# The causal mask as a third matmul, and a LayerNorm that reads PSUM, in a hybrid decoder layer

## The chip, the cores and the metric

The kernel runs on one core of one Trainium2 chip. The metric is the device time of one execution in microseconds; the time before is the median of three runs. The engines are called PE (matrix products and transposes; PEld is its loading of weights), DVE (the vector engine), ACT (activations), POOL (GpSimd) and SP (the queue that issues most of the transfers).

## The reference

One decoder layer over 2048 tokens of width 1024, in float32. Half of the mixer is a convolution branch, the other half is an attention without softmax; a SwiGLU follows.

```python
glu = val * jax.nn.sigmoid(gate)                    # 512 channels
y = causal depthwise convolution of glu, width 31, + conv_b
y = _layernorm(y, ln_g, ln_b)                       # over the 512 channels
conv_out = jax.nn.silu(y)

z = einsum("bhqd,bhkd->bhqk", q, k) / 8             # 8 heads of 64
mask = key_pos < q_pos                              # a token does not read itself
log_beta, log_1m_beta = log_sigmoid(z), where(mask, log_sigmoid(-z), 0)
between = reverse_cumsum(log_1m_beta) - log_1m_beta
attn = where(mask, exp(log_beta + between), 0)      # = sigmoid(z) * prod of (1 - sigmoid)
attn_out = headwise_rmsnorm(attn @ v)

h = x + rmsnorm(concat(conv_out, attn_out) @ w_out)
h = h + rmsnorm(swiglu(rmsnorm(h)) @ w_down)        # hidden width 2816
```

## The kernel before

Tokens are worked on in four groups `g` of 512. Products keep float32 accuracy by splitting each operand into a high and a low part (`H` on ACT, `L` as the difference on DVE or POOL) and adding three matmuls into one PSUM bank.

**The first 1510 us or so** hold three streams that are recorded side by side. The dense stream is the list `PLAN`: `qkv` and `gv` (input projection, `dense`, L253, L255, L257), `out` (output projection, L684 to L686), and the first products of the feed-forward part (`c11` and `p4`, L755). Beside it run `attn` and `taps` (the convolution: 31 multiply-adds on DVE for each block of channels, L468 and L473, in a PSUM bank of the tag `cv`), each to the share of its work that `ATTN` and `TAPS` name for a place in the plan. After about 1510 us only feed-forward products are left, all on L755.

**The attention** sweeps each head's keys in chunks of 512 from the diagonal back. One score step (`scores`) handles 128 queries against one chunk: two matmuls (L558, L559) fill a bank `z`, of which there are two; ACT takes two sigmoids of it (`om` on L564, `A` on L566); DVE turns `om` into a running product (the scan on L568); POOL multiplies the two (L569). One chunk later (`values`) PE transposes `A` (L585), ACT and DVE split it (`TH` on L245, `TL` on L246) and two matmuls add to `o` (L590, L591). The scan reads one element of `z` as an operand, so the bank is held from its first matmul to the end of the scan. In a chunk on the diagonal the step is only as wide as the keys that can be seen, 128 to 512, and DVE adds -1e30 to the upper triangle of its last 128 columns (L561) before ACT reads it. There are 320 steps: 32 for group 0 (all on the diagonal), 64, 96 and 128 for the others, 32 on the diagonal in each; so 128 masks in all. Below, steps are counted from 0 in the order in which they stand on PE.

**The convolution's end** (`convnorm`) takes 128 tokens at a time, 16 times in all: PE turns the block into the `cv` bank (L486, name `lps`), ACT copies the bank to the tile `cy` (L488), DVE takes mean and variance from the copy (L490, L492), POOL makes the inverse root (L188, L189), DVE subtracts the mean and multiplies by the gain (L494), then multiplies by the inverse root and adds the offset (L495). Four score steps later PE turns the result back through the same bank (L503, `cps`); there is one `cv` bank.

What is recorded is then sorted for each engine by the framework's scheduler, which plays the program through on estimated durations; only the taps and the late feed-forward part are held in the recorded order. So each engine runs a fixed list, and an edit in one place can move rows in the lists of all of them.

Of the kernel before, what the change touches and what calls it, by code (L numbers as in the profile page):

```python
# [9 lines left out]
F32 = mybir.dt.float32  # L10
F32R = mybir.dt.float32r
BF16 = mybir.dt.bfloat16
AF = mybir.ActivationFunctionType
ALU = mybir.AluOpType
# [4 lines left out]
P = 128  # L19
# [116 lines left out]
def layer_kernel(ctx: ExitStack, tc: tile.TileContext, x, xT, g_pre_mix, w_in, conv_w, conv_b, ln_g, ln_b,  # L136
                 attn_g, w_out, g_post_mix, g_pre_ffn, w_gate, w_up, w_down, g_post_ffn, out):
    nc = tc.nc
# [7 lines left out]
    idr = cp.tile([P, P], F32R, name="idr")  # L146
# [9 lines left out]
    def const(pool, name, src, shape):  # L156
        t = pool.tile(shape, F32, name=name)
        waiting.append((t, src))
        return t
# [12 lines left out]
    def ev(name, dt=F32, n=G):  # L172
        return rp.tile([P, n], dt, tag="ev", name=name, bufs=4)
# [10 lines left out]
    def rstd_of(dst, ss, n, tag="ms"):  # L184

        w = dst.shape[-1]
        m = sp.tile([P, 8], F32, tag=tag, name=tag, bufs=4)
        nc.gpsimd.tensor_scalar(m[:, 0:w], ss, 1.0 / n, EPS, ALU.mult, ALU.add)  # L188
        nc.gpsimd.tensor_tensor(dst, m[:, 0:w], nhalf[:, 0:w], ALU.pow)  # L189
# [69 lines left out]
    def to_col(rows, k, Hs, Ls, g, banks=bank):  # L259

        ps = banks("tps")
        for t in range(TT):
# [10 lines left out]
    cc = ctx.enter_context(tc.tile_pool(name="mixconsts", bufs=1))  # L273
# [9 lines left out]
    lng = const(cc, "lng", ln_g.partition_broadcast(P), [P, CH])  # L283
# [3 lines left out]
    ident = ev("ident")[:, 0:P]  # L287
    make_identity(nc, ident)
    nc.vector.tensor_copy(idr, ident)
    msk = cc.tile([P, P], F32, name="msk")  # L290
    nc.gpsimd.memset(msk, NEG)
    nc.gpsimd.affine_select(msk, msk, pattern=[[1, P]], compare_op=ALU.is_ge, fill=0.0, base=0,
                            channel_multiplier=-1)
    one = cc.tile([P, 1], F32, name="one")
    nc.gpsimd.memset(one, 1.0)

# [163 lines left out]
    def taps(g):  # L460

        acc = vp.tile([P, CB, G], F32, tag="acc", name="acc", bufs=1)
        conv[g] = dp.tile([P, CB, G], F32, name=f"conv{g}")
        for c in range(CB):
            yield need(("val", g, c))
            a = pp.tile([P, G], F32, tag="cv", name="cv", bufs=1)
            tc.keep_in_program_order(
                nc.vector.tensor_scalar(a, gl[c][:, 0:G], cw[:, c, 0:1], cb_[:, c:c + 1], ALU.mult, ALU.add))  # L468
            yield 1
            for k in range(1, CW):  # L470
                to = acc[:, c, :] if k == CW - 1 else a
                tc.keep_in_program_order(
                    nc.vector.scalar_tensor_tensor(to, gl[c][:, k:k + G], cw[:, c, k:k + 1], a, ALU.mult, ALU.add))  # L473
                yield 1
            done.add(("taps", g, c))
        for _ in range(TAPLAG):
            yield 3
        yield from convnorm(g, acc)

    def convnorm(g, acc):  # L480

        for t in range(TT):
            ts_ = slice(t * P, (t + 1) * P)
            ps = pp.tile([P, G], F32, tag="cv", name="lps", bufs=1)
            for c in range(CB):
                nc.tensor.transpose(ps[:, c * P:(c + 1) * P], acc[:, c, ts_], id32)  # L486
            y = vp.tile([P, CH], F32, tag="cy", name="cy", bufs=1)
            nc.scalar.activation(y, ps, AF.Copy)  # L488
            st = sp.tile([P, 6], F32, tag="st", name="st")
            nc.vector.bn_stats(st, y)  # L490
            mv = sp.tile([P, 3], F32, tag="mv", name="mv")
            nc.vector.bn_aggr(mv[:, 0:2], st)  # L492
            rstd_of(mv[:, 2:3], mv[:, 1:2], 1, "msc")
            nc.vector.scalar_tensor_tensor(y, y, mv[:, 0:1], lng, ALU.subtract, ALU.mult)  # L494
            nc.vector.scalar_tensor_tensor(y, y, mv[:, 2:3], lnb, ALU.mult, ALU.add)  # L495
            s = vp.tile([P, CH], F32, tag="cs", name="cs", bufs=1)
            nc.scalar.activation(s, y, AF.Sigmoid)
            nc.gpsimd.tensor_tensor(s, y, s, ALU.mult)
            for _ in range(LAG):
                yield 3  # L500
            pt = pp.tile([P, G], F32, tag="cv", name="cps", bufs=1).rearrange("p (c t) -> p c t", c=CB)
            for c in range(CB):
                nc.tensor.transpose(pt[:, c, :], s[:, c * P:(c + 1) * P], id32)  # L503
            r = s.rearrange("p (c t) -> p c t", c=CB)
            nc.scalar.activation(r, pt, AF.Copy)
            nc.scalar.dma_start(conv[g][:, :, ts_], r)
        done.add(("conv", g))
# [22 lines left out]
    def attn(g):  # L530
# [20 lines left out]
        def scores(u, j):  # L551
            hd_ = heads[u["h"]]
            diag = u["c"] == g
            w = (j + 1) * P if diag else G
            K = u["K"]
            z = pp.tile([P, G], F32, tag="z", name="z")
            js = slice(j * P, (j + 1) * P)
            nc.tensor.matmul(z[:, 0:w], hd_["QL"][:, js], K[:, 0:w], start=True, stop=False)  # L558
            nc.tensor.matmul(z[:, 0:w], hd_["QH"][:, js], K[:, 0:w], start=False, stop=True)  # L559
            if diag:  # L560
                nc.vector.tensor_tensor(z[:, w - P:w], z[:, w - P:w], msk, ALU.add)  # L561
            om = ap.tile([P, G + 1], F32, tag="om", name="om", bufs=NOM)
            nc.gpsimd.tensor_copy(om[:, G:G + 1], hd_["prev"][j])
            nc.scalar.activation(om[:, G - w:G], z[:, 0:w], AF.Sigmoid, scale=-0.125)  # L564
            a = ap.tile([P, G], F32, tag="A", name="A", bufs=NA)
            nc.scalar.activation(a[:, 0:w], z[:, 0:w], AF.Sigmoid, scale=0.125)  # L566
            r = om[:, G - w:G + 1][:, ::-1]
            nc.vector.tensor_tensor_scan(r, r, z[:, 0:1].to_broadcast([P, w + 1]), one, ALU.mult, ALU.bypass)  # L568
            nc.gpsimd.tensor_tensor(a[:, 0:w], a[:, 0:w], om[:, G - w + 1:G + 1], ALU.mult)  # L569
            pv = sp.tile([P, 1], F32, tag="pv", name="pv", bufs=8)  # L570
            nc.gpsimd.tensor_copy(pv, om[:, G - w:G - w + 1])
            hd_["prev"][j] = pv
            u["A"].append(a)
            return w
# [56 lines left out]
        for n in range(len(units) + 1):  # L631
            u = None
            if n < len(units):
                h, c = units[n]
                if c == g:
                    yield need(("q", g, h // 2), ("k", g, h // 2), ("v", g, h // 2))
                    heads[h] = begin(h)
                u = fetch(h, c)
            for i in range(TT):
                w = 0  # L640
                if u is not None:
                    w += scores(u, i)
                if last is not None:
                    w += values(last, i)
                later = [(k - 1, fn, a) for k, fn, a in later]
                while later and later[0][0] <= 0:
                    _, fn, a = later.pop(0)
                    if fn is back and g > 1:
                        yield need(("mix", g - 2))
                    fn(a)  # L650
                yield w
            if last is not None and last["c"] == 0:
                h = last["h"]
                oT = ap.tile([P, G], F32, tag="oT", name="oT", bufs=1)
                nc.scalar.activation(oT, heads[h]["o"], AF.Copy)
                heads[h]["oT"] = oT
                later.append((FOLD, fold_halves, h))
                if h % 2:
                    later.append((BACK, back, h))
            last = u  # L660
# [721 lines left out]
```

## Time and profile before

| | before |
|---|---|
| median of 3 runs | 2632.16 us (2631.33 to 2634.64) |
| the profiled execution, and its span | 2632.4 us, 2630.6 us |
| mean granted PE clock | 0.97 |
| PE, DVE, ACT, POOL busy (share of the span) | 94%, 71%, 49%, 56% |
| first and last score step | 88.0 us, 1503.2 us |
| data moved | 657.32 MB, 250 GB/s |

A busy PE is the time in which at least one matmul is under way; matmuls overlap, so a record is longer than the distance to the next one. The granted clock is 1 when PE runs at its full rate and 0.5 when the throttle halves it. In a table of stretches each engine's number is its busy time within the stretch, and in brackets the instructions.

### The profile page before, as it was taken

To read this page: it belongs to the slowest core of one execution; us is meant where nothing else is said; L and a number is where in the kernel's file an instruction comes from. 1 tells how busy PE (TensorE), PEld (TensorE's weight loads), DVE (VectorE), ACT (ScalarE), POOL (GpSimd) and SP (SyncE) were. 2 spreads that over 40 slices of the span, in tenths; PEclk is the share of its full clock that TensorE was granted. 3 is DMA by queue.
4 is the path that set the end of the run, shared out by engine and by line. 5 is a ranking of instruction groups with operands and counts; after the bars stand their busy time and mean duration, and the time that the engine had idled before them with its cause. 6 is when DMAs were issued, how large, how long until landed. Compare 5 with 4: busy or idle time off the path is not lost.

```text
span 2630.6 us, 35776 instructions
## 1 busy us (share of the span) xinstructions
PE 2460.1 (94%) x11156; PEld 1970.1 (75%) x11156; DVE 1859.7 (71%) x2409; ACT 1290.7 (49%) x2395; POOL 1482.0 (56%) x1844
## 2 busy tenths in 40 slices
PE   8889989997999999999999989889999999999998
PEld 6777867785777778777788767667777777887886
DVE  5787569977999676687765538877776665557556
ACT  4455546656564565557666643333322224444543
POOL 6654587557765656548534406675534434557556
PEclk9999989998999999989999989999999999999999
DMA  9999869986798788856777646887665557668654
GB/s 343 330 305 308 286 221 314 358 285 219 255 350 262 251 306 277 293 168 224 264 255 231 203 152 216 315 270 242 206 210 184 193 199 271 194 196 271 210 190 170
DMA packets 289182, 657.32 MB, mean 250 GB/s; under 512 B 33888, under 2 KB 42080, under 8 KB 288992
## 3 DMA queue, kind: packets, MB, share of 16 engines
q1 hardware_dynamic: 264704, 622.01, 70.8%
q10 hardware_dynamic: 24288, 33.04, 3.5%
q8 instruction: 88, 1.44, 0.2%
q14 instruction: 102, 0.84, 0.1%
HBM read 460.92 MB, written 193.99 MB: 249 GB/s over the span
## 4 chain that ended last, share of the span: by engine, by line
PE 61%; DVE 15%; DMA 10%; POOL 6%; issue 5%; ACT 2%; SPq 1%; POOLq 0%; DVEq 0%; ACTq 0%
PE b L755 16%; PE dps L755 13%; PE c L755 9%; DVE om L568 3%; PE at L585 3%; DVE cv L473 2%; PE inps L253 2%; PE inps L255 2%; PE inps L257 2%; PE p L755 2%; PE o L591 2%; PE z L558 2%; PE ops L686 1%; PE ops L684 1%; PE ops L685 1%
## 5 line engine op out<-in xcount | busy, mean ns | idle before, releaser
L569 POOL TENSOR_TENSOR A<-A,om 128x512 f32<-128x512 f32 (+2 forms) x320 | 314.4, 983 | 356.5 <-DVE om L568 314.8
L568 DVE TENSOR_TENSOR_SCAN om<-om,one,z 128x513 f32<-128x513 f32 (+2 forms) x320 | 351.5, 1112 | 115.1 <-ACT A L566 103.1
L1061 POOL TENSOR_TENSOR wL<-raw,wH 128x512 fp32r<-128x512 f32 x176 | 257.2, 1489 | 283.7 <-ACT wH L1060 283.7
L473 DVE SCALAR_TENSOR_TENSOR cv<-glu,cw,cv 128x512 f32<-128x512 f32 x464 | 346.4, 746 | 5.8
L1241 DVE TENSOR_TENSOR xL__22087<-t__22089,xH__22086 128x512 fp32r<-128x512 f32 x154 | 197.8, 1293 | 159.2 <-ACT xH__22086 L1240 159.2
L1239 POOL TENSOR_TENSOR xL__22085<-t__22088,xH__22084 128x512 fp32r<-128x512 f32 x154 | 207.6, 1353 | 176.1 <-ACT xH__22084 L1238 175.5
L253 PE MATMUL inps<-xH,wL 128*128 128x512 f32 x640 | 262.2, 410 | 4.3 <-DVE qkL L246 4.0
L255 PE MATMUL inps<-xH,wH 128*128 128x512 f32 x640 | 259.0, 405 | 0.0
L257 PE MATMUL inps<-xL,wH 128*128 128x512 f32 x640 | 258.6, 405 | 0.0
L564 ACT ACTIVATE om<-z 128x512 f32<-128x512 f32 (+2 forms) x320 | 171.0, 536 | 164.9 <-DVE z L561 67.3
L246 DVE TENSOR_TENSOR TL<-at,TH 128x512 fp32r<-128x512 f32 (+1 forms) x320 | 189.2, 598 | 85.4 <-ACT TH L245 84.7
L755 PE MATMUL dps<-xH__22084,xL__22087 128*128 128x512 f32 x616 | 241.6, 392 | 6.8 <-DVE xL__22087 L1241 5.6
L755 PE MATMUL dps<-xL__22085,xH__22086 128*128 128x512 f32 x616 | 241.3, 392 | 3.9 <-POOL xL__22085 L1239 3.9
L755 PE MATMUL dps<-xH__22084,xH__22086 128*128 128x512 f32 x616 | 241.0, 391 | 0.0
L839 POOL TENSOR_TENSOR sum<-sum 128x512 f32<-128x512 f32 x132 | 172.2, 1305 | 104.3 <-DMA sum<-in_w_down_dram 37.5
L207 ACT ACTIVATE wH<-raw 128x1024 fp32r<-128x1024 f32 x156 | 165.6, 1062 | 104.1 <-DMA raw<-in_w_in_dram 42.7
L245 ACT ACTIVATE TH<-at 128x512 fp32r<-128x512 f32 (+1 forms) x320 | 167.7, 543 | 90.8 <-PE at L585 82.5
L1238 ACT ACTIVATE xH__22084<-t__22088 128x512 fp32r<-128x512 f32 x154 | 97.1, 631 | 232.8 <-POOL xL__22085 L1239 145.0
L585 PE MATMUL at<-idr,A 128*128 128x128 f32 x1088 | 194.2, 283 | 10.9 <-ACT ma L625 3.6
L585 PEld LDWEIGHTS at<-idr,A 128*128 128x128 f32 x1088 | 143.7, 146 | 48.8 <-POOL A L569 5.9
L566 ACT ACTIVATE A<-z 128x512 f32<-128x512 f32 (+2 forms) x320 | 167.5, 537 | 21.3 <-PE at L585 19.6
L558 PE MATMUL z<-K,QL 128*128 128x512 f32 (+2 forms) x320 | 132.4, 415 | 29.4 <-DVE om L568 24.0
(303 smaller groups left out, 6283.3 us busy)
## 6 DMA issues: line engine op xcount, KB each, us to landing
wL<-wL SPq DMA_DIRECT2D x156, 512.0 KB, 4.7
raw<-in_w_in_dram SPq DMA_DIRECT2D x80, 512.0 KB, 5.9
t__22089<-u SPq DMA_DIRECT2D x154, 256.0 KB, 2.8
c<-c ACTq DMA_DIRECT2D x88, 256.0 KB, 3.9
t__22088<-wd SPq DMA_DIRECT2D x88, 256.0 KB, 2.9
K<-kd SPq DMA_DIRECT2D x80, 256.0 KB, 4.5
V<-vd SPq DMA_DIRECT2D x80, 256.0 KB, 4.1
u<-accf SPq DMA_DIRECT2D x22, 768.0 KB, 4.1
```

The costliest lines, as they stand in the source:

```text
L246: nc.vector.tensor_tensor(L, ps, H.bitcast(F32), ALU.subtract)
L253: nc.tensor.matmul(ps, WL[:, kc], aH[t](k), start=k == 0, stop=False)
L255: nc.tensor.matmul(ps, WH[:, kc], aH[t](k), start=False, stop=False)
L257: nc.tensor.matmul(ps, WH[:, kc], aL[t](k), start=False, stop=k == KT - 1)
L473: nc.vector.scalar_tensor_tensor(to, gl[c][:, k:k + G], cw[:, c, k:k + 1], a, ALU.mult, ALU.add))
L568: nc.vector.tensor_tensor_scan(r, r, z[:, 0:1].to_broadcast([P, w + 1]), one, ALU.mult, ALU.bypass)
L569: nc.gpsimd.tensor_tensor(a[:, 0:w], a[:, 0:w], om[:, G - w + 1:G + 1], ALU.mult)
L585: nc.tensor.transpose(pt[:, j * P:(j + 1) * P], u["A"][j][:, b * P:(b + 1) * P], id32)
L755: return nc.tensor.matmul(ps, a, b, skip_group_check=True, **flags)
L1061: nc.gpsimd.tensor_tensor(l, t, f32(h), sub)
L1239: nc.gpsimd.tensor_tensor(WL, w, f32(WH), sub)
L1241: nc.vector.tensor_tensor(UL, t, f32(UH), sub)
```

## The change

The mask becomes an operand of PE. It is built in a short-lived tile, rounded once to PE's format (`mskr`), and a third matmul with the identity `idr` as the other operand adds it into the last 128 columns of the bank; the addition on DVE goes. In `convnorm` the copy to `cy` goes, and the statistics and the first of the two DVE operations read the PSUM bank `lps`.

```diff
-    msk = cc.tile([P, P], F32, name="msk")
+    mskr = cc.tile([P, P], F32R, name="mskr")
+    msk = ev("msk")[:, 0:P]
     nc.gpsimd.memset(msk, NEG)
     nc.gpsimd.affine_select(msk, msk, pattern=[[1, P]], compare_op=ALU.is_ge, fill=0.0, base=0,
                             channel_multiplier=-1)
+    nc.vector.tensor_copy(mskr, msk)
...
             y = vp.tile([P, CH], F32, tag="cy", name="cy", bufs=1)
-            nc.scalar.activation(y, ps, AF.Copy)
             st = sp.tile([P, 6], F32, tag="st", name="st")
-            nc.vector.bn_stats(st, y)
+            nc.vector.bn_stats(st, ps)
             mv = sp.tile([P, 3], F32, tag="mv", name="mv")
             nc.vector.bn_aggr(mv[:, 0:2], st)
             rstd_of(mv[:, 2:3], mv[:, 1:2], 1, "msc")
-            nc.vector.scalar_tensor_tensor(y, y, mv[:, 0:1], lng, ALU.subtract, ALU.mult)
+            nc.vector.scalar_tensor_tensor(y, ps, mv[:, 0:1], lng, ALU.subtract, ALU.mult)
...
-            nc.tensor.matmul(z[:, 0:w], hd_["QH"][:, js], K[:, 0:w], start=False, stop=True)
+            nc.tensor.matmul(z[:, 0:w], hd_["QH"][:, js], K[:, 0:w], start=False, stop=not diag)
             if diag:
-                nc.vector.tensor_tensor(z[:, w - P:w], z[:, w - P:w], msk, ALU.add)
+                nc.tensor.matmul(z[:, w - P:w], idr, mskr, start=False, stop=True)
```

The scheduler's lists change with it. From the first score steps on, rows change places on every engine; in the late feed-forward part all lists read as before. Lines after the diff's first place read one to three higher in the changed kernel.

On DVE, in the first group's steps, the list reads before (z is masked, `om` is the scan, `TL` and `qkL` are low parts, `cv` is a tap):

```order
L561 TENSOR_TENSOR z<-z,msk 128x128
L568 SCALAR_TENSOR_TENSOR om<-om,one,z 128x385
L568 SCALAR_TENSOR_TENSOR om<-om,one,z 128x513
L561 TENSOR_TENSOR z<-z,msk 128x128
L246 TENSOR_TENSOR qkL<-inps,qkH 128x512
L568 SCALAR_TENSOR_TENSOR om<-om,one,z 128x129
L561 TENSOR_TENSOR z<-z,msk 128x128
L568 SCALAR_TENSOR_TENSOR om<-om,one,z 128x257
L246 TENSOR_TENSOR TL<-at,TH 128x512
L473 SCALAR_TENSOR_TENSOR cv<-glu_134,cw,cv 128x512
```

and now, at the same place:

```order
L569 SCALAR_TENSOR_TENSOR om<-om,one,z 128x385
L569 SCALAR_TENSOR_TENSOR om<-om,one,z 128x513
L569 SCALAR_TENSOR_TENSOR om<-om,one,z 128x129
L246 TENSOR_TENSOR qkL<-inps,qkH 128x512
L569 SCALAR_TENSOR_TENSOR om<-om,one,z 128x257
L246 TENSOR_TENSOR TL<-at,TH 128x512
L475 SCALAR_TENSOR_TENSOR cv<-glu_136,cw,cv 128x512
```

The masks are gone and what stood between them has moved together.

On PE, at the third group's second head (steps 122 and 123), where the output projection of the second group begins, before:

```order
L558 MATMUL z<-K,QL 128x384
L559 MATMUL z<-K,QH 128x384
L585 MATMUL at<-idr,A 128x128 x2
L558 MATMUL z<-K,QL 128x512
L559 MATMUL z<-K,QH 128x512
L590 MATMUL o<-TH,V 128x512
L591 MATMUL o<-TL,V 128x512
L590 MATMUL o<-TH,V 128x512
L585 MATMUL at<-idr,A 128x128 x4
L591 MATMUL o<-TL,V 128x512
L585 MATMUL at<-idr,A 128x128 x4
L684 MATMUL ops<-wH,xL 128x512
```

and now:

```order
L562 MATMUL z<-mskr,idr 128x128
L592 MATMUL o<-TL,V 128x512
L586 MATMUL at<-idr,A 128x128 x3
L559 MATMUL z<-K,QL 128x384
L560 MATMUL z<-K,QH 128x384
L562 MATMUL z<-mskr,idr 128x128
L685 MATMUL ops<-wH,xL 128x512
L686 MATMUL ops<-wH,xH 128x512
L687 MATMUL ops<-wL,xH 128x512
```

The mask matmul stands behind its pair (121 of the 128 stand directly behind it), and the projection's products (`ops`) begin one step earlier. The run of steps without any dense matmul between them was 105 to 122 and is 108 to 121.

On PE, at the last group's second head (step 215), where the feed-forward products `c` fill in, before:

```order
L558 MATMUL z<-K,QL 128x512
L559 MATMUL z<-K,QH 128x512
L590 MATMUL o<-TH,V 128x512
L591 MATMUL o<-TL,V 128x512
L590 MATMUL o<-TH,V 128x384
L585 MATMUL at<-idr,A 128x128 x2
L755 MATMUL c_12501<-xH,wL 128x512
L755 MATMUL c_12501<-xH,wH 128x512
L755 MATMUL c_12501<-xL,wH 128x512
```

and now:

```order
L559 MATMUL z<-K,QL 128x512
L560 MATMUL z<-K,QH 128x512
L591 MATMUL o<-TH,V 128x512
L592 MATMUL o<-TL,V 128x512
L591 MATMUL o<-TH,V 128x384
L586 MATMUL at<-idr,A 128x128 x2
L592 MATMUL o<-TL,V 128x384
L607 MATMUL pf<-idr,oT 128x128 x4
L591 MATMUL o<-TH,V 128x256
```

The `c` products have moved ahead of this place. The second run of steps without dense matmuls was 220 to 226 and is 214 to 226.

## The prediction

> **What bounds the kernel now.** I read the page first: engine shares, slices, and the chain that ended last.
>
> ```profile
> PE 2460.1 (94%) x11156; PEld 1970.1 (75%) x11156; DVE 1859.7 (71%) x2409; ACT 1290.7 (49%) x2395; POOL 1482.0 (56%) x1844
> PE   8889989997999999999999989889999999999998
> DVE  5787569977999676687765538877776665557556
> PEclk9999989998999999989999989999999999999999
> PE 61%; DVE 15%; DMA 10%; POOL 6%; issue 5%; ACT 2%; SPq 1%; POOLq 0%; DVEq 0%; ACTq 0%
> ```
>
> PE is the bound overall, and the change gives it work. But 15% of the chain is DVE, and DVE reaches 9 in slices 7, 8 and 11 to 13, in the score part, where the change takes work from it. So the question is asked stage by stage. Next I cut the score part (88 to 1510 us) where the character changes:
>
> ```profile
> 88.00:231.00 143.00, 127.60 (x602) 103.76 (x602) 119.57 (x206) 75.61 (x161) 78.95 (x133) 0.93 0.97 322
> 231.00:314.00 83.00, 79.92 (x397) 65.79 (x398) 47.01 (x75) 44.12 (x86) 48.65 (x77) 0.98 0.87 285
> 314.00:485.00 171.00, 153.88 (x701) 123.25 (x700) 139.68 (x194) 97.03 (x183) 131.14 (x181) 0.92 0.83 288
> 485.00:600.00 115.00, 110.26 (x544) 89.40 (x542) 95.29 (x146) 58.47 (x113) 58.95 (x102) 1.00 0.90 301
> 600.00:673.00 73.00, 57.46 (x253) 41.45 (x254) 62.94 (x93) 46.45 (x94) 55.54 (x94) 0.88 0.67 209
> 673.00:757.00 84.00, 79.10 (x386) 64.08 (x385) 80.05 (x110) 51.52 (x92) 64.21 (x90) 1.00 0.89 300
> 757.00:828.00 71.00, 63.23 (x285) 48.92 (x283) 68.48 (x103) 37.22 (x75) 38.23 (x67) 0.90 0.91 302
> 828.00:1104.00 276.00, 270.21 (x1332) 219.54 (x1331) 182.53 (x242) 162.29 (x295) 165.51 (x237) 0.99 0.83 280
> 1104.00:1142.00 38.00, 30.19 (x104) 19.44 (x105) 35.25 (x51) 22.25 (x44) 19.20 (x35) 0.73 0.72 233
> 1142.00:1510.00 368.00, 357.70 (x1760) 289.40 (x1759) 253.22 (x335) 239.97 (x448) 179.71 (x334) 1.00 0.69 228
> ```
>
> Columns: stretch, its length, busy PE, PEld, DVE, ACT, POOL, then granted clock, DMA share, GB/s. Two kinds show. In 231-314, 485-600, 673-757, 828-1104 and 1142-1510 PE is 94 to 98% busy at a clock of 0.98 to 1.00: PE-bound, 926 us in all. In 88-231, 314-485, 600-673, 757-828 and 1104-1142 PE is 79 to 90% busy, its clock is down to 0.93 to 0.73, and DVE is 82 to 96% busy: here PE waits, and what it waits for runs over DVE. Idle PE there is 15.4, 17.1, 15.5, 7.8 and 7.8 us, 63.6 together. The masks in the same stretches, in the same order:
>
> ```profile
> 88.00:231.00 143.00, 9.01 (x32) 0.93 0.97 322
> 231.00:314.00 83.00, 2.37 (x8) 0.98 0.87 285
> 314.00:485.00 171.00, 4.62 (x16) 0.92 0.83 288
> 485.00:600.00 115.00, 3.45 (x12) 1.00 0.90 301
> 600.00:673.00 73.00, 2.22 (x8) 0.88 0.67 209
> 673.00:757.00 84.00, 1.18 (x4) 1.00 0.89 300
> 757.00:828.00 71.00, 2.22 (x8) 0.90 0.91 302
> 828.00:1104.00 276.00, 4.61 (x16) 0.99 0.83 280
> 1104.00:1142.00 38.00, 1.06 (x4) 0.73 0.72 233
> 1142.00:1510.00 368.00, 5.88 (x20) 1.00 0.69 228
> ```
>
> So 60 masks lie in PE-bound stretches, 68 in those where PE waits. The groups by line and form:
>
> ```profile
> L561 DVE TENSOR_TENSOR z<-z,msk 128x128 f32<-128x128 f32 x128 | 36.6, 291 | 48.0 <-PE z L559 47.9
> L473 DVE SCALAR_TENSOR_TENSOR cv<-glu,cw,cv 128x512 f32<-128x512 f32 x464 | 346.4, 746 | 5.8
> L494 DVE SCALAR_TENSOR_TENSOR cy<-cy,mv,lng 128x512 f32<-128x512 f32 x16 | 14.8, 925 | 0.7
> L490 DVE BATCH_NORM_STATS2 st<-cy 128x6 f32<-128x512 f32 x16 | 11.0, 688 | 8.1 <-ACT cy L488 8.0
> ```
>
> **The sum, against the profiled execution (2632.4 us; the median of the runs is 2632.16, the same within 0.3).**
>
> *The mask matmul.* It isn't in the trace, but the first `z` matmul of a diagonal step has its form, 128 by 128 in the same type, amid dense matmuls (start, own duration):
>
> ```profile
> 100.12 0.40 PE L253 MATMUL inps<-xH,wL 128*128 128x512 f32 x1
> 100.35 0.22 PE L558 MATMUL z<-K,QL 128*128 128x128 f32 x1
> 100.41 0.27 PE L559 MATMUL z<-K,QH 128*128 128x128 f32 x1
> 100.52 0.45 PE L255 MATMUL inps<-xH,wH 128*128 128x512 f32 x1
> 100.81 0.39 PE L257 MATMUL inps<-xL,wH 128*128 128x512 f32 x1
> ```
>
> From L253 to L257 are 0.69 us, for two of 512 columns (0.23 each: 100.12 to 100.35) and two of 128: 0.115 us for one. Bounds: 0 where PE idles anyway, 128 x 0.115 = 14.7 us if every one is in the way. I take the full price for the 60 in PE-bound stretches, **+6.9**, and nothing for the 68 others, 7.8 us which the 63.6 us of idle PE hide; if that idle goes, up to 7.8 comes back. The matmul adds no wait: both operands are there from the start, and 121 of 128 stand directly behind their pair.
>
> [...]
>
> *The addition that goes.* 0.291 us of DVE each. In 88-231 all 32 steps are masked; DVE is 84% busy, and waits for the masks' own input too:
>
> ```profile
> ACT om L564 <- DVE z L561: 18.5, 11, 5.5
> DVE z L561 <- PE z L559: 13.1, 5, 5.3
> ```
>
> (who waits for whom, us, times, longest; in 88-231.) DVE's list loses 9.0 us of work there, and 13.1 us of waiting in line that may only move to the scan. I count **-9.0**; bounds 0 and -22.1. In the four other waiting stretches 36 masks free 10.1 us of DVE. DVE is the late one for a part only (82 to 96% busy, while transfers and POOL stand in the chain too), so I count half, **-5.0**; bounds 0 and -10.1. In PE-bound stretches freed DVE time is worth nothing: PE does not wait there.
>
> *The clock.* The waiting stretches lose (1 - clock) x length: 10.0 us in 88-231, and 13.7, 8.8, 7.1 and 10.3 in the others. If 9.0 of 15.4 us idle go, 5.9 of the 10.0 would go in proportion; if 5.0 of 48.2, 4.1 of 39.9. Half of the sum, since the half rate comes in blocks: **-5.0**; bounds 0 and -10.
>
> *The moved order.* Score steps without any dense matmul between them (counted in the lists) are where PE starves. They were 105 to 122 and 220 to 226, and become 108 to 121 and 214 to 226: the first run loses four, the second gains six. Stretch 600-673 is the first run, 18 steps: 15.5 idle plus 8.8 of clock, 1.35 us for a step. Two more cost **+2.7**; bounds -1.4 (the first run's shortening alone counts in part) and the rival below.
>
> *The LayerNorm.* Sixteen copies leave ACT (no wait of PE hangs on ACT's load there), DVE no longer waits 8.0 us for them, and the subtraction may fall from 925 ns, reading two SBUF tiles, to 746, the tap that reads one from PSUM: 2.9 us. The blocks end in 231-314, 485-673, 828-1104 and 1142-1510, mostly where DVE is 57 to 69% busy: **0**; bounds -10.9 and +2. The one `cv` bank is held through three DVE operations instead of one copy, but its next user is four score steps off, 4.4 us each (1422 us for 320); only a DVE later than that would uncover it. The statistics now wait for the transposes on PE; behind them in DVE's list stand scans, with the same 8.0 us as the bound.
>
> [...]
>
> *At the start* one cast of the mask, at most an addition's 0.29 us, beside the first loads: 0.
>
> Sum: +6.9 - 9.0 - 5.0 - 5.0 + 2.7 = -9.4, so **2623 us**.
>
> **The rivals.** *PE pays in full.* DVE's relief turns into waiting at its next row, the scan, which already waits for ACT more than the mask waited for PE:
>
> ```profile
> DVE om L568 <- ACT A L566: 103.1, 71, 5.4
> DVE z L561 <- PE z L559: 47.9, 37, 5.3
> ACT om L564 <- DVE z L561: 67.3, 46, 5.5
> ```
>
> Then nothing is gained, and all 128 matmuls push: 2632.4 + 14.7 = 2647. It decides if PE's idle in the waiting stretches stays at 63.6 us although the masks are gone. For it speaks the chain's 61% PE; against it ACT's 67.3 us behind the mask, a whole engine hop that goes. That the change fails to do what it says would look the same: ACT's first sigmoid would then wait as long for PE as it did for DVE.
>
> *The second dry run.* In 1104-1142 the seven steps 220 to 226 and their surroundings lost 7.8 us idle and 10.3 of clock, 2.6 for a step. Six more at that price, less 4 x 1.35 for the first run, are +10.2 instead of +2.7: 2631, no change. It needs the clock to fall as low as 0.73 again, over 13 steps. [...]
>
> *A larger gain.* In 88-231 DVE's 13.1 us of waiting go with the work, and the other stretches keep all 10.1: -22.1 - 10.1 + 6.9 + 2.7, with -10 of clock, gives -32.6, 2600. The 23.4 us that DVE idles in 88-231 speak against: other waits stand right behind.
>
> **How the numbers follow.** A difference within 0.2% (5.3 us) can't be told from no change. The forecast case (2614 to 2627) has 0.42, the larger gain 0.12, the second dry run or an even balance 0.25, PE paying in full 0.14, and dry run and PE together, near 2657, 0.07. So faster 0.53, same 0.26, slower 0.21. The range runs from 2605, most of the way to the larger gain, to 2648, which takes in PE paying in full.
>
> **What would show it.** After the change the stretch of the first 32 steps should be about 9 to 14 us shorter, DVE there without L561, its wait for `A` at the scan grown by less than 13 us. The PE-bound stretches should grow by 0.115 us for each mask. The steps 214 to 226 should show a clock of 0.7 to 0.8 for longer than the 38 us of now, and the first dry run should be shorter. The feed-forward part after the last step should take what it takes now. I am wrong if the first 32 steps take as long as before, or if PE's idle beside the scan's wait grows by what the mask released.

## The result, and the profile after

| | before | after |
|---|---|---|
| median of 5 runs | 2632.16 us (2630.92 to 2634.64) | 2645.96 us (2642.65 to 2653.19) |
| profiled execution, and its span | 2632.4 us, 2630.6 us | 2645.96 us, 2644.2 us |
| first and last score step | 88.0 us, 1503.2 us | 87.4 us, 1519.7 us |

The changed kernel is slower: the ratio of the times is 1.0052, with a 95% interval from 1.0041 to 1.0064, or 13.8 us. The forecast was 2623, on the other side; 2646 lies inside its range only because the range reached up to the rival in which PE pays in full. The page after (engine shares, the slices of PE, DVE and PE's clock, the chain that ended last):

```profile
PE 2469.5 (93%) x11284; PEld 1983.0 (75%) x11284; DVE 1818.0 (69%) x2282; ACT 1283.0 (49%) x2379; POOL 1476.0 (56%) x1844
PE   8989989997999999989999979889999999998998
DVE  5686478977799655787675537877776675557556
PEclk9999999998999999999999989999999999999999
PE 42%; DVE 6%; POOL 4%; issue 2%; DMA 2%; ACT 1%; SPq 0%; POOLq 0%; DVEq 0%; ACTq 0%
```

DVE has lost the 41.7 us that the change takes from it (1859.7 to 1818.0). The chain says little here: its shares sum to under 60%, so it was not followed to the start. What follows the last score step took 1127.4 us before and 1124.5 us after, so all of the loss lies in the 320 score steps. They are one stretch in each kernel (length, busy PE, PEld, DVE, ACT, POOL, clock, DMA share, GB/s). Before:

```profile
88.00:1503.20 1415.20, 1324.91 (x6335) 1062.38 (x6335) 1079.08 (x1541) 831.36 (x1580) 837.18 (x1339) 0.96 0.82 272
```

After:

```profile
87.40:1519.70 1432.30, 1334.95 (x6463) 1075.36 (x6463) 1036.99 (x1413) 822.02 (x1563) 828.28 (x1339) 0.97 0.79 267
```

PE is busy for 10.0 us more, with 128 more matmuls. It also idles for 7.1 us more (90.3 to 97.4), although DVE, for which it used to wait, has 42 us less to do. That is the surprise: the work went, and the waiting grew. Who waits for whom, us, times, longest; first rows of before, in the order of the answer:

```profile
DVE TL L246 <- ACT TH L245: 84.7, 61, 4.4
...
POOL sum L839 <- DMA sum<-in_w_down_dram: 37.5, 16, 7.5
...
POOL sum L839 <- DMA sum<-in_w_gate_dram: 23.8, 10, 8.2
...
POOL sum L839 <- DMA sum<-in_w_up_dram: 23.2, 12, 5.0
...
DVE cy L495 <- POOL mv L189: 16.1, 10, 3.5
```

and the same of after:

```profile
DVE TL L246 <- ACT TH L245: 146.9, 76, 6.1
DVE om L569 <- ACT A L567: 117.6, 68, 6.5
...
POOL sum L840 <- DMA sum<-in_w_down_dram: 43.3, 23, 4.9
...
POOL sum L840 <- DMA sum<-in_w_up_dram: 37.4, 14, 6.4
...
DVE cy L496 <- POOL mv L189: 32.6, 10, 6.7
...
POOL sum L840 <- DMA sum<-in_w_gate_dram: 28.4, 10, 6.1
```

DVE's wait for `A` at the scan grew by 14.5 us, its wait for `TH` by 62.2. Two rows that no term of the forecast had looked at grew too. POOL waits longer at `sum` (sums of feed-forward weights, background work that POOL does among the score steps, each from tiles that SP loads into three buffers), and DVE waits twice as long in the convolution's LayerNorm for POOL's inverse root.

### The profile page after: what moved, and what is told of

Same layout as the page of the kernel before. It is cut to its first block, busy times and chain, and to the rows that moved or that the text cites. A ratio compares the mean times of both kernels' runs of the same rounds, so it can differ in the third digit from the quotient of the medians.

```text
span 2644.2 us, 35830 instructions
## 1 busy us (share of the span) xinstructions
PE 2469.5 (93%) x11284; PEld 1983.0 (75%) x11284; DVE 1818.0 (69%) x2282; ACT 1283.0 (49%) x2379; POOL 1476.0 (56%) x1844
## 4 chain that ended last, share of the span: by engine, by line
PE 42%; DVE 6%; POOL 4%; issue 2%; DMA 2%; ACT 1%; SPq 0%; POOLq 0%; DVEq 0%; ACTq 0%
PE b L756 16%; PE dps L756 13%; PE c L756 5%; PE p L756 2%; DVE accf L1069 1%; PE at L586 1%; PE ops L687 1%; PE ops L685 1%; PE ops L686 1%; PE o L592 1%; POOL wL L1062 1%; PE o L591 1%; PE z L559 1%; PE z L560 1%; POOL xL__22071 L1240 1%
## 5 line engine op out<-in xcount | busy, mean ns | idle before, releaser
L257 PE MATMUL inps<-xL,wH 128*128 128x512 f32 x640 | 258.4, 405 | 0.0
```

The lines of the kernel that those rows point to most:

```text
L257: nc.tensor.matmul(ps, WH[:, kc], aL[t](k), start=False, stop=k == KT - 1)
```

## The experiments

All ratios are against runs of the kernel before on the same chip; the runs were made on several chips, so times are compared by these ratios. The profile of a kernel is one execution.

### The change with the lists kept

The scheduler had moved rows on every engine. To part the edit from this, the rows of each engine are tied in the order that the kernel before has, with edges that order two instructions and make none wait. A mask matmul stands directly behind its pair, the rows that go are left out (code shortened):

```diff
     layer_kernel(tc, *args)
+    for e, rows in ORDER_BEFORE.items():          # PE, DVE, ACT, POOL, SP
+        for a, b in zip(rows, rows[1:]):
+            tc.add_manual_dep(b, a.name, NoSync)  # b stands behind a
```

Mask alone, tied (m_pin):

> The mask alone on PE, the LayerNorm as before, and every engine's list tied to the order that the kernel before has, with each mask matmul directly behind its pair. If PE pays in full wherever the mask stands (128 x 0.115 us, DVE's relief turned into other waiting): 2640 to 2647. If the loss came from the rearranged lists, the forecast's own terms hold here without the dry-run term (-9.0 - 5.0 - 5.0 + 6.9 = -12): 2617 to 2626. If the LayerNorm part was the loss: at or below 2632.

LayerNorm alone, tied (ln_pin):

> The LayerNorm part alone (statistics and subtraction read PSUM, no copy on ACT), the mask on DVE, and the lists tied to the order of the kernel before. If this part costs nothing by itself: 2630 to 2634. If holding the one bank through three DVE operations, or the statistics' wait for PE, is the loss: 2638 or more. Its bounds in the prediction were -10.9 and +2.

Both, tied (full_pin):

> Both parts, with the lists tied to the order of the kernel before. If the rearranged lists are the loss: 2617 to 2630, well under the changed kernel's 2646. If PE pays in full: 2640 to 2647, as the changed kernel. The difference to the changed kernel is what the order alone is worth.

Mask alone, sorted anew (m_free):

> The mask alone on PE, the LayerNorm as before, and the lists sorted anew by the scheduler. If the masks cost PE in full: 2640 to 2647. If the mask's rearrangement is the loss, it lies as far above the mask with tied lists as the changed kernel lies above both with tied lists. If the LayerNorm part is the loss: 2632 or less.

LayerNorm alone, sorted anew (ln_free):

> The LayerNorm part alone, the mask on DVE, and the lists sorted anew. With tied lists this part measured 0.9998. If any new sorting of the lists costs, 1.002 to 1.008, although nothing costly was changed. If only the mask's sorting costs: 0.999 to 1.001. Its second run of steps without dense matmuls is 216 to 226 instead of 220 to 226, as long as most of the changed kernel's: if that is what the changed kernel loses by, about +8 us or 1.003.

| | tied to the old order | sorted anew |
|---|---|---|
| mask | 0.9999 [0.9987, 1.0012] | 1.0064 [1.0041, 1.0087] |
| LayerNorm | 0.9998 [0.9985, 1.0011] | 0.9996 [0.9984, 1.0008] |
| both | 0.9985 [0.9971, 0.9998] | 1.0052 (the changed kernel) |

With its lists kept the whole change is not slower: 2625.89 us beside 2629.45, a ratio whose interval barely leaves 1, and each half alone stays at 1. The two kernels of the last row have the same rows and differ in their order (and in the semaphore instructions that the framework places by it: 35830 and 35794 instructions in all), and that is worth 0.0067, or 17.6 us (the two intervals together give about 4.7 either way). All of the loss is the order. (The kernel before with its own order tied was not run; the LayerNorm part tied, 0.9998, shows no sign that the ties themselves gain.) The score steps of the tied kernel:

```profile
87.90:1501.00 1413.10, 1333.82 (x6462) 1075.55 (x6462) 1049.16 (x1412) 822.89 (x1563) 829.04 (x1339) 0.97 0.81 273
```

Here PE is 8.9 us busier than before and idles for 79.3 us instead of 90.3. Beside it PE in the changed kernel is busy for only 1.1 us more but idles 18.1 us more (79.3 to 97.4): the order costs idle PE. What PE waited for in the score steps, first in the changed kernel:

```profile
PE z L559 <- DVE om L569: 34.9, 47, 2.0
...
PE at L586 <- POOL A L570: 9.6, 6, 5.3
```

then in the tied one:

```profile
PE z L559 <- DVE om L569: 25.9, 36, 2.3
...
PE at L586 <- POOL A L570: 3.1, 5, 1.2
```

PE waits for the scans of the score steps more often, and longer for POOL's products. This is where the loss shows, not yet what makes them late.

### The two prices

```diff
-                nc.tensor.matmul(z[:, w - P:w], idr, mskr, start=False, stop=True)
+                for i in range(3):
+                    nc.tensor.matmul(z[:, w - P:w], idr, mskr, start=False, stop=i == 2)
```

> Both parts with the lists tied to the order of the kernel before, and each mask added three times on PE (256 more matmuls of 128 columns; the sigmoid of the masked places stays zero). Against both parts with tied lists, 0.9985 of before. If PE pays for every mask wherever it stands: +29.4 us, about 1.0097. If only the masks in PE-bound stretches cost: +13.8, about 1.0038. If PE has the time: 0.9985.

It measured 1.0040 [1.0027, 1.0053]. Against both parts tied that is 0.0055, 14.5 us for 256 matmuls (about 5 either way): 0.057 us for one, where 0.115 would be the full pitch. So about half of their time reaches the end, as the forecast had counted (60 of 128). The first mask of a step has the same pitch as these two. One step of the LayerNorm part alone and the same step with both parts, lists tied in both (start, duration):

```profile
241.03 0.39 PE L558 MATMUL z<-K,QH 128*128 128x512 f32 x1
241.26 0.39 PE L255 MATMUL inps<-xH,wH 128*128 128x512 f32 x1
241.49 0.40 PE L257 MATMUL inps<-xL,wH 128*128 128x512 f32 x1
```

```profile
243.21 0.40 PE L560 MATMUL z<-K,QH 128*128 128x512 f32 x1
243.44 0.22 PE L562 MATMUL z<-mskr,idr 128*128 128x128 f32 x1
243.50 0.45 PE L255 MATMUL inps<-xH,wH 128*128 128x512 f32 x1
243.78 0.40 PE L257 MATMUL inps<-xL,wH 128*128 128x512 f32 x1
```

From the start of the second `z` matmul to that of L257 are 0.46 and 0.57 us. At all four widths the median over the steps in which PE does not wait is the same: 0.11 us more with one mask, and 0.22 more again with two further ones. If half of that reaches the end for the first mask too, the 128 cost about 7.3 us.

```diff
                 nc.vector.tensor_tensor(z[:, w - P:w], z[:, w - P:w], msk, ALU.add)
+                nc.vector.tensor_tensor(z[:, w - P:w], msk, z[:, w - P:w], ALU.add)
```

> The kernel before with each mask added twice on DVE, the second time directly behind the first, and the lists tied to the order of the kernel before: 128 x 0.291 = 37.2 us more on DVE. It is the forecast's DVE term with the opposite sign. If freed DVE time is worth what the forecast said (9.0 for the 32 masks of the first steps, half of 10.1 for 36 others, nothing for 60, the clock 5.0): +14 to +19 us, about 1.0062, and the first 32 steps 9 us longer. If DVE's time is worth what the tied lists with the mask on PE suggest (7 to 11 us): about 1.0035. If DVE's time is worth nothing anywhere: within 0.0015 of before.

It measured 1.0063 [1.0041, 1.0086], 16.6 us (about 6 either way), in the middle of what the forecast's DVE terms say with the sign turned. But taking the same work away seems to give less: the mask with tied lists stayed at before's time, so DVE's relief there was about as much as the 7.3 us that PE pays, and with the LayerNorm part some 11 (about 4 either way). The first 32 steps suggest why. With the LayerNorm part alone, the mask still on DVE, the stretch is

```profile
88.80:227.70 138.90, 127.13 (x602) 102.76 (x602) 120.20 (x207) 75.37 (x161) 78.37 (x133) 0.95 0.99 331
```

and DVE's waits in it

```profile
DVE z L560 <- PE z L558: 11.2, 5, 5.0
DVE om L567 <- ACT A L565: 3.7, 2, 2.9
DVE qkL L246 <- ACT qkH L245: 2.8, 1, 2.8
DVE TL L246 <- ACT TH L245: 1.7, 2, 1.4
```

With the mask alone on PE the stretch is

```profile
89.70:228.60 138.90, 128.23 (x635) 105.19 (x635) 114.11 (x174) 75.28 (x161) 78.92 (x133) 0.96 0.98 323
```

and DVE's waits in it

```profile
DVE om L570 <- ACT A L568: 6.8, 6, 3.8
DVE qkL L246 <- ACT qkH L245: 5.9, 2, 3.0
DVE TL L246 <- ACT TH L245: 5.6, 6, 2.5
DVE vt L246 <- ACT vt L245: 2.4, 2, 2.0
```

Both take 138.9 us. DVE does 6.1 us less, and the 11.2 us that it waited at the mask for PE come back as waits for ACT in the rows behind. The other two kernels with this order give 143.2 (before) and 141.8 (both parts tied): a gain of 0 and of 1.4 us, where single executions with the mask on the same engine differ by 3 to 4. With two masks on DVE the same steps took 147.9:

```profile
87.50:235.40 147.90, 130.24 (x603) 104.74 (x603) 127.59 (x239) 76.12 (x161) 79.02 (x133) 0.93 0.97 317
```

That is 9.0 us more than with the LayerNorm part alone and 4.7 more than before, for 9.3 us of work. So more work on DVE pushed the end here, and less work let ACT and PE be the late ones. With one execution of each this is suggested, not shown; and the second addition also stands in the chain from `z` to ACT's sigmoid, so that DVE's time and the longer chain are not told apart.

### The order by itself

Four tiny copies, 128 by 1, behind scans of one head of the first group; the scheduler then sorts the lists anew (code shortened):

```diff
+            if diag and g == 0 and u["h"] == 4:
+                nc.vector.tensor_copy(idle, z[:, 0:1])
             hd_["prev"][j] = pv
```

> The kernel before with four more DVE copies of one column (well under 0.1 us each) behind the scans of group 0's fifth head, and the lists sorted anew: 2,900 of PE's rows change places, among them the second run of steps without dense matmuls, 216 to 226 instead of 220 to 226. If the order by itself is worth tenths of a per cent, this differs from before by more than its interval, to either side, 0.996 to 1.008; if only the changed instructions matter, it is the same within 0.0015.

With `u["h"] == 0` in all groups, sixteen copies:

> The kernel before with sixteen such copies (four in the first head of each group), lists sorted anew: the first run of steps without dense matmuls becomes 104 to 130 instead of 105 to 122, nine steps longer, the second stays 220 to 226. By 1.35 us for a step it should be 12 us slower, about 1.0046. If the length of that run does not matter: within 0.0015 of before; if the order decides by something else: any ratio from 0.996 to 1.008.

In the changed kernel, four copies, with `g == 0` and `u["h"] == 2`:

> The changed kernel with four more DVE copies of one column behind the scans of group 0's third head, lists sorted anew: its second run of steps without dense matmuls is 220 to 226 again, as in the kernel before, and the first 107 to 122. If that run is what the changed kernel loses by (1.5 us for each of six steps): about 9 us less than the changed kernel's 1.0052, so 1.0018. If the order is worth something all over, not there alone: any ratio from 0.998 to 1.008.

And both parts of the change, tied to another order that was made for the mask on DVE:

> Both parts, all lists tied to another order that was sorted for the mask on DVE: that of the LayerNorm part alone, which measured 0.9996. Each mask matmul stands directly behind its pair. If the mask on PE is by itself neutral to slightly good on any list: 0.997 to 1.001. If what tied lists showed holds for the order of the kernel before only: 1.002 or more.

They measured 1.0063 [1.0049, 1.0077], 1.0015 [1.0003, 1.0027], 1.0059 [1.0041, 1.0077] and 1.0006 [0.9995, 1.0016]. The first is the plainest: four copies that do nothing, of 0.13 us each (I had expected under 0.1), in a kernel that else is the one before, cost as much as the whole change, because rows change places: their own 0.53 us is far too little. The second has the longest first dry run (score steps without a dense matmul between them) of all, 27 steps, and loses 4 us where 1.35 us for a step would make 12. The third has the old second dry run back and is no faster than the changed kernel (the mask alone, sorted anew, has it too, at 1.0064), and the LayerNorm part sorted anew has most of the new one and loses nothing. So the length of the dry runs, by which the forecast priced the order, does not tell the loss. The fourth says that the change costs nothing clear of noise on a second kept order either.

### Whose list

Only some engines' lists are tied (code shortened):

```diff
-    for e, rows in ORDER_BEFORE.items():
+    for e, rows in ORDER_BEFORE.items() if e in TIED:
```

PE's list tied, all others free (full_pe):

> Both parts, with PE's list alone tied to the order of the kernel before and the other engines' lists sorted by the scheduler. All lists tied gave 0.9985, none tied 1.0052. If what is lost lies in PE's order: 0.998 to 1.000. If it lies in the other engines' lists: 1.003 to 1.006.

PE's free, all others tied (full_rest):

> Both parts, with DVE's, ACT's, POOL's and SP's lists tied to the order of the kernel before and PE's sorted by the scheduler. PE then follows closely (1,200 of 11,159 rows stand elsewhere). If the loss needs the other lists to move too: 0.998 to 1.000. If PE's own moves are enough: 1.002 or more.

POOL's and SP's free (pool_sp_free):

> Both parts, with PE's, DVE's and ACT's lists tied to the order of the kernel before, and POOL's and SP's sorted by the scheduler. With PE's list alone tied the ratio was 1.0063, with all tied 0.9985. POOL waits at the sums of the feed-forward weights (L840) for their transfers, 88 us before, 91 with all lists tied, 103 to 122 in the kernels with a ratio over 1.005. If the loss is that POOL and SP have the sums and their transfers at worse places: 1.003 to 1.007, with POOL's wait there over 100 us. If it lies in DVE's and ACT's order: 0.998 to 1.001.

DVE's and ACT's free (dve_act_free):

> Both parts, with PE's, POOL's and SP's lists tied, and DVE's and ACT's sorted by the scheduler. If the loss lies with POOL and SP: 0.998 to 1.001, and POOL's wait at the sums stays near 91 us. If it lies in DVE's and ACT's order: 1.003 to 1.007.

| lists left to the scheduler | ratio | POOL's wait at `sum` for transfers |
|---|---|---|
| none | 0.9985 [0.9971, 0.9998] | 91 us |
| PE | 1.0007 [0.9992, 1.0021] | 98 us |
| DVE, ACT | 1.0008 [0.9993, 1.0022] | 91 us |
| POOL, SP | 1.0037 [1.0022, 1.0051] | 85 us |
| DVE, ACT, POOL, SP | 1.0063 [1.0044, 1.0081] | 103 us |
| all | 1.0052 [1.0041, 1.0064] | 117 us |

PE's own order is not what loses: with it kept and the rest free the kernel is as slow as the changed one. POOL and SP carry the larger part, yet the waits at `sum` did not grow there as I had expected (85 us). Against all tied, POOL with SP lose 0.0052 and DVE with ACT 0.0023; all four together lose 0.0078, about the sum. The kernel with only PE's list tied shows one stall at `sum` whole, since its PE rows match those of the tied kernel. Its POOL, DVE and PE (start, duration, idle before and what ended it):

```profile
592.08 1.30 POOL L840 TENSOR_TENSOR sum<-sum 128x512 f32<-128x512 f32 x1 [7.93 <-DMA sum<-in_w_up_dram]
593.82 1.28 POOL L840 TENSOR_TENSOR sum<-sum 128x512 f32<-128x512 f32 x1 [0.43 <-DMA sum<-in_w_up_dram]
...
596.22 1.26 POOL L840 TENSOR_TENSOR sum<-sum 128x512 f32<-128x512 f32 x1
...
597.96 0.55 POOL L189 TENSOR_TENSOR mv<-msc,nhalf 128x1 f32<-128x1 f32 x1
...
598.54 1.57 DVE L496 SCALAR_TENSOR_TENSOR cy<-cy,mv,lnb 128x512 f32<-128x512 f32 x1 [6.05 <-POOL mv L189]
600.03 1.27 DVE L569 TENSOR_TENSOR_SCAN om<-om,one,z 128x513 f32<-128x513 f32 x1
...
594.23 0.36 PE L591 MATMUL o<-TH,V 128*128 128x256 f32 x1
601.36 0.80 PE L559 MATMUL z<-K,QL 128*128 128x512 f32 x1 [6.76 <-DVE om L569]
```

It is read from the top: POOL stands at a sum for a transfer, three sums, this one included, lie ahead of the inverse root, DVE stands for that at the LayerNorm with the scan behind it, and PE stands for the scan's bank; ACT, too, waits 6.8 us for DVE's row. Four engines stand behind one transfer of background work, 7.93 us on POOL, 6.05 on DVE, 6.8 on ACT and 6.76 on PE. With all lists tied two sums fewer lie there, and the stall is shorter:

```profile
592.16 1.28 POOL L840 TENSOR_TENSOR sum<-sum 128x512 f32<-128x512 f32 x1 [4.97 <-DMA sum<-in_w_up_dram]
...
595.10 0.55 POOL L189 TENSOR_TENSOR mv<-msc,nhalf 128x1 f32<-128x1 f32 x1
...
595.68 1.57 DVE L496 SCALAR_TENSOR_TENSOR cy<-cy,mv,lnb 128x512 f32<-128x512 f32 x1 [3.41 <-POOL mv L189]
```

### The transfers of the sums

The lists tied, but one kind of row moved on SP alone (the edit in words):

```diff
 # SP's rows: t = piece(...)  ->  dma_start(t, w[j][:, e * G:(e + 1) * G])
+each of the 132 loads up to six rows later, not past a store of a sum     (sums_late)
+each up to four, or two, rows earlier, not past a load or store of a sum  (sums_early4, sums_early2)
```

> Both parts, all lists tied to the order of the kernel before, but each of SP's 132 loads for the sums stands up to six rows later on SP (3.2 on average, never past a row that stores a sum). Nothing else moves. If POOL's wait for these loads holds up the steps: POOL's wait at the sums goes over 110 us and the ratio to 1.002 to 1.006. If the wait is only a sign of something else: 0.998 to 1.000 although the wait grows.

> Both parts, all lists tied to the order of the kernel before, but each of SP's 132 loads for the sums stands up to four rows earlier on SP (1.2 on average, not past another load or store of the sums). POOL still waits 91 us at the sums with tied lists. If the loads' place on SP is what holds POOL: the wait falls under 80 us and the ratio under 0.9985, to 0.993 to 0.998. If the loads must wait for one of the three tiles to come free, SP stands still there and what is queued behind comes later: 1.000 or more.

> The same with at most two rows earlier (0.8 on average). If the loads' place is what holds POOL: between 0.995 and 0.9985. If free tiles are lacking: 0.9985 to 1.002.

3.2 rows later on average cost 1.0502 [1.0484, 1.0520], some 131 us, far over what I expected; in its profile the first score step starts at 112.0 us instead of 87.9, and the steps take 1520.1 us instead of 1413.1. POOL's idle time ahead of the sums (us, times):

```profile
  DMA sum<-in_w_gate_dram: 114.6, 18
  DMA sum<-in_w_up_dram: 85.6, 17
  DMA sum<-in_w_down_dram: 78.6, 17
```

So late transfers of the sums do reach the end, and the order of the transfers on SP is the most sensitive thing found here. Earlier is not better, though only 66 of the loads found room to move: 1.0040 [1.0028, 1.0052] and 1.0038 [1.0023, 1.0053]. Both lose before the steps: the first score step starts at 95.5 and 93.0 us instead of 87.9. The 320 steps take 1414.8 and 1425.5 us beside the tied kernel's 1413.1; but the three profiled executions lie 2.6 us under, 8.6 over and 3.6 over the medians of their kernels, so how much more is lost in the steps stays open. The wait at `sum` stayed at 83 and 88 us in them. Whether a better place for these loads exists in the score part alone was not tried.

What stays open is which rows lose the 17.6 us in the changed kernel itself. It is shown that the order does, that mostly the lists of engines other than PE carry it, that in the changed kernel it ends as idle PE, most of all at `z` for DVE's scan, and that a transfer of a sum can stall four engines; no single row or wait accounts for it.

The one version found that beats both kernels is both parts with tied lists, 0.9985, and its interval barely leaves 1.

## Why the prediction was wrong, point by point

The step that failed is the price of the moved order, 2.7 us where 17.6 were lost; and the gain from DVE's freed time was put about twice too high.

- *The mask matmul, +6.9*: right as a sum. About 7.3 us for 128, by the price of 0.057 us each (an estimate: that half of the first masks' time reaches the end, as with the further ones, was not measured). The split was not so sharp: cut at the steps nearest to the forecast's times, the 256 further masks made the PE-bound stretches 8.4 us longer and the others 3.8 (one execution each), where the forecast's count gives 13.8 and nothing.
- *The addition that goes, -9.0 in the first 32 steps*: failed. At a kept order 0 and 1.4 us were gained there, inside the spread of single executions. The term took the 84% of DVE for a bound in both directions; here other waits stood right behind, as the forecast had noted for its larger rival only. The changed kernel's first 32 steps are 6.7 us shorter (143.2 to 136.5), close to the sign that I had named, but the kernel with the mask on DVE and tied lists shows 4.3 of it as well, and that with the four copies, mask on DVE and 1.0063, has 136.7. The sign did not part the cases.
- *The other stretches and the clock, -5.0 and -5.0*: with the term above the forecast had -19; the tied lists give between 7 and 11 (about 4 either way). In the waiting stretches, cut by step as above, PE idled 61.2 and 60.0 us with the mask on DVE (before, ln_pin) and 57.1 and 53.8 with it on PE (m_pin, full_pin): some 5 us less, where 14.0 were forecast. In the PE-bound ones, where freed DVE time was to be worth nothing, it fell too, from 29.1 and 28.8 to 25.0 and 25.5. The clock over the steps was 0.961 and 0.966, then 0.975 and 0.967. So the direction was right, the size about twice too large, and the place only in part. That the half rate comes in blocks is in the trace of before: the clock is 0.50 in, for instance, 90 to 94, 170 to 174, 625 to 631 and 1130.5 to 1140 us, and 1.00 in 96 to 166 and 632 to 650.
- *The moved order, +2.7*: this is the step that turned the sign. It measured 17.6. The forecast looked at one feature of PE's list, the runs of steps without dense matmuls, and gave each step a price. The loss lies mostly in the other lists, and kernels with long and short runs came out fast and slow alike. The price, 1.35 us for a step, was misread besides: 600 to 673 us holds steps 106 to 128, and the run ends with step 122, at 645 us.
- *The LayerNorm, 0*: right, 0.9998 (though DVE is 83 to 86% busy in 485 to 673 us, not 57 to 69). The subtraction from PSUM took what was forecast from the tap's row (746), and the statistics took 694 ns out of PSUM beside 688 out of SBUF. No run shows the bound of +2 us: the 16 statistics took 11.1 us in all where they had taken 11.0, and the 16 subtractions 12.0 where they had taken 14.8:

```profile
L495 DVE SCALAR_TENSOR_TENSOR cy<-lps,mv,lng 128x512 f32<-128x512 f32 x16 | 12.0, 747 | 0.5
...
L491 DVE BATCH_NORM_STATS2 st<-lps 128x6 f32<-128x512 f32 x16 | 11.1, 694 | 5.6 <-PE lps L488 5.5
```

- *The rivals.* "PE pays in full" gave 2647, and the time is 2646, but not for its reason: half of the matmuls are paid, and without the moved rows the kernel is no slower than before: that the range took the time in is luck. Its first half, DVE's relief turning into waits for ACT, is what the first 32 steps look like. "The second dry run" fell with the copies that brought the old run back and left the time at 1.0059; and its sign, a clock of 0.7 to 0.8 for longer than 38 us, did not come: steps 214 to 226 took 35.0 us at 0.81 (before 43.4 us at 0.88).
- *What I said would show me wrong* was PE's idle time beside the scan's wait growing by what the mask released. Both grew, by 7.1 and 14.5 us, if by less than that, but the test cannot tell masks from order: it needs a kernel with the order kept.

## What to carry to other kernels

Where a scheduler sorts the lists, an edit is two changes, and they are to be measured apart: tie the new kernel's rows in the old kernel's order, and only then ask what the edit is worth. A tuned kernel's order is itself part of the tuning, and here every new sorting but one was worse, by 0.15 to 0.64%; so a gain forecast below about half a per cent is not a forecast until the order is fixed. And a high busy share, here DVE's 84% in the first 32 steps, may price work that is added (9.3 us more made them 4.7 us longer than before, and 9.0 longer than with the LayerNorm part alone), but here it did not price work that is taken away (the 9.0 us of the masks, for 0 and 1.4 us at a kept order; one execution of each): for that, look which engine is late next in the same rows.

## What the runs showed that I had not expected

- Four copies of one column, 0.53 us together, moved the time by 16.6 us (1.0063), through the order of the rows.
- Moving 132 loads by 3.2 rows on the queue that issues them cost 131 us (1.0502), while the data moved are the same.
- 256 matmuls of 128 columns, each directly behind a matmul into the same bank, cost 0.057 us each in the time of the kernel (about 0.02 either way), half of the 0.11 us by which each moves the rows behind it, at 94% busy PE.
